# A hybrid decoder step on one core: convolution and gate at projection eviction, second-dilation keys in residue order, four stationary columns for the denominators

## The chip, the cores and the metric

The kernel runs on one core of a Trainium2 chip. The metric is the device time of one execution in microseconds (us), lower is better. The kernel before took 2710.33 us (median of three runs, 2706.25 to 2712.09). A profiled execution gives, for each engine, when each instruction ran and what it waited for. The engines are PE (TensorE: matmuls, and PEld for the weight loads that run beside them), DVE (VectorE), ACT (ScalarE), POOL (GpSimd) and SP, which here issues most DMA transfers. Each works off its own instructions strictly in order.

## The reference

One step of a decoder layer: 2048 new prompt tokens (and 64 sample tokens, which the change hardly touches). A combined projection feeds two branches: attention over three dilations (window 128 step 1, 512 step 4, 2048 step 16), and a state-space branch (a causal convolution of width 4, SiLU, then chunks of 128 tokens). Both are merged by an output projection and followed by an MLP.

```python
q, k, v, z, xbc, dt_raw = jnp.split(rmsnorm(h, norm_mix) @ w_in, IN_SPLITS, axis=-1)
groups = [dilated_group_prompt(q, k, v, d, w // d) for (w, d) in ((128, 1), (512, 4), (2048, 16))]
att = combine_groups(groups)                 # softmax over the union of the three windows
y = conv_b
for tap in range(4):                         # causal convolution along the tokens
    y = y + ext[:, tap:tap + s] * conv_w[tap]
xbc = silu(y)                                # x, B, C of the state-space branch
y, h_final = ssd_chunked(x, dt, A, B, C, h0) # 16 chunks of 128 tokens, one state carried over
y = (y + d_skip * x) * silu(z)               # z's gate, then a grouped RMS norm
h = h + concat([att, ssm]) @ w_out
h = h + (relu(rmsnorm(h) @ w_up) ** 2) @ w_down
```

## The kernel before, in words

All data is fp32. A large matmul is done as three: operands are split into a high part (rounded on ACT) and a low part (the rest, subtracted on DVE), and high x high, high x low and low x high are summed (`mm3`, lines 177 to 181; `mm`, lines 1124 to 1127). A scheduler orders the instructions of each engine when the program is built: it takes them by priority, which is the order of the code, but an instruction whose inputs or whose buffer are not yet there is passed over. That order is then fixed, and a tile's buffer can be used again when all readers of the former tile are done. So the code's order, the number of buffers and the place of a pool in memory together set the queues.

The work comes in five stretches.

1. **First projections** (lines 284 to 432). Eight blocks of 256 tokens give q, k, v and z. `z_part` computes four tiles of z per block, copies them from PSUM (L425) and stores them raw to `xz_s[8:12]` from ACT's queue (L426). Tiles `ev` and `kf` share two buffers.
2. **Attention** (the loop of 16 steps, 4 key heads x 4 blocks `s` of 512 tokens). `att_a` computes scores: `qk` (L609) multiplies keys, split in `kA` and `kB`, with queries. Dilation 1 takes 128 adjacent keys as the stationary operand, dilation 4 takes every fourth key (`slice(t0, t0 + 4 * 127 + 1, 4)`), dilation 16 every sixteenth (`att_qk3`). `att_b` subtracts the maximum, exponentiates, splits, sums the denominators by a matmul (`den_mm`, L696, which multiplies 128 columns of `rows_r`, only some of them ones, with 512 probabilities) and multiplies with the values (L749). `att_c` does the third dilation's values (L780) once per head. The other projection tiles, `ps_xz` (x, B and C: 8 tiles of 128 channels for each of the 8 blocks, `g2`), are placed between the attention matmuls as filler, held back by the table `STEP`; the last `LATE = 6` blocks of tiles 4 to 7 are code of the stretch after attention. `g2` copies a tile from PSUM (L811) and stores it raw.
3. **Hand-over**. The denominators are stored, loaded again (`dent`, L909), added, inverted and stored (`r_s`, L914); `merge` loads the attention outputs (`am`, L1060) and the inverses (`rd`, L1064), adds and multiplies them (L1073 to L1078) and splits the result into `mix`.
4. **First four chunks** of the state-space branch (`branch(0, ...)`), with the rest of the filler. `ssd_load` loads a chunk's raw x, B, C with three tokens of history (`xc`), the decays (`ar`), z (`zt`) and `ea`, two buffers each. `ssd` convolves on ACT and DVE (one ACT instruction L958 and three DVE instructions L960 for each of 8 channel tiles), applies SiLU (L970 tanh, L971), gates z (L972 tanh, L973), transposes (`ps_xt`, L977), multiplies the decays with C x B (L993), computes `ps_y` (L997), updates the state (`hst`), adds the skip (L1023), multiplies with the gate (L1024, POOL), norms (L1027 to L1041, matmuls `ps_ss` L1033 and L1038) and splits into `mix`.
5. **Output projection and MLP** (`out`, `up`, `down`), four passes of 512 tokens, from the first `ps_o` that needs the merged `mix`. The other twelve chunks and the sample tokens run beside the MLP's matmuls.

## Time and profile before

| of the profiled execution | value |
|---|---|
| its own time; its span in the trace | 2705.8 us; 2704.1 us |
| PE busy | 2582.9 us (96%) |
| DVE busy | 1650.8 us (61%) |
| ACT busy | 1146.5 us (42%) |
| POOL busy | 471.8 us (17%) |
| matmuls | 15382 |
| mean granted clock of PE | 0.979 |
| DMA, mean over the span | 172 GB/s |

Busy time is the time in which an engine executes. Matmuls are pipelined, so a busy PE can still have matmuls follow each other at different pitches; the pitch, start to start, is what a matmul costs. The chain that ended last is 69% PE. A wait is put down to the last thing that released it.

### The profile page before, as it was taken

How to read it: one execution, taken by the hardware profiler on the slowest of the kernel's cores; microseconds unless marked ns; L12 is line 12 of the kernel's file. 1: busy time of each engine (PE TensorE's matmuls, PEld its weight loads, DVE VectorE, ACT ScalarE, POOL GpSimd, SP SyncE). 2: the span in 40 equal slices, each digit the busy share in tenths (PEclk: the TensorE clock that was granted, in tenths of full speed). 3: DMA queues.
4: the chain of work that ended last, by engine and by line, in shares of the span. 5: the costliest groups of instructions: out<-in, count | busy, mean ns of one | idle time of the engine just before them, and what ended most of it. 6: DMA issues, size and time to landing. Idle time of an engine off the chain costs nothing.

```text
span 2704.1 us, 42090 instructions
## 1 busy us (share of the span) xinstructions
PE 2582.9 (96%) x15382; PEld 2268.9 (84%) x15382; DVE 1650.8 (61%) x2917; ACT 1146.5 (42%) x2203; POOL 471.8 (17%) x406
## 2 busy tenths in 40 slices
PE   7999789989956999999999999999999999999998
PEld 7999789989955777888888887777788889999998
DVE  6444357777767646777558775445667664555455
ACT  5334234555543434444454443343444434333333
POOL 2222124545612110010121010020000113000000
PEclk9999899999977999999999999999999999999999
DMA  7666768876693744544465446476644434433322
GB/s 262 190 207 211 206 204 238 223 233 186 210 261 97 224 133 156 160 146 139 164 210 168 149 141 196 159 227 221 187 141 153 148 119 146 161 102 103 109 98 86
DMA packets 346942, 464.56 MB, mean 172 GB/s; under 512 B 39264, under 2 KB 227104, under 8 KB 345696
## 3 DMA queue, kind: packets, MB, share of 16 engines
q1 hardware_dynamic: 302992, 425.24, 50.6%
q10 hardware_dynamic: 43744, 36.65, 4.2%
q8 instruction: 121, 1.98, 0.3%
q14 instruction: 85, 0.70, 0.1%
HBM read 366.25 MB, written 129.09 MB: 183 GB/s over the span
## 4 chain that ended last, share of the span: by engine, by line
PE 69%; DMA 3%; DVE 1%; issue 1%; ACT 0%; POOL 0%; SPq 0%; DVEq 0%; POOLq 0%; ACTq 0%
PE ps_dn L1124 9%; PE ps_up L1124 9%; PE ps_up L1126 9%; PE ps_dn L1127 9%; PE ps_dn L1126 9%; PE ps_up L1127 9%; PE ps_o L1124 2%; PE ps_o L1126 2%; PE ps_o L1127 2%; PE ps_po L1570 1%; PE ps_xz L177 1%; PE ps_xz L180 1%; PE ps_xz L181 1%; PE ps_yo L1003 1%; PE ps_y L997 0%
## 5 line engine op out<-in xcount | busy, mean ns | idle before, releaser
L899 ACT ACTIVATE wm_h<-raw_m 128x512 fp32r<-128x512 f32 x576 | 362.3, 630 | 791.8 <-PE ps_dn L1126 442.1
L900 DVE TENSOR_TENSOR wm_l<-raw_m,wm_h 128x512 fp32r<-128x512 f32 x576 | 415.7, 723 | 106.9 <-ACT wm_h L899 95.9
L1124 PE MATMUL ps_up<-xh_m,wm_h 128*128 128x512 f32 (+1 forms) x1280 | 458.5, 358 | 0.0
L1124 PE MATMUL ps_dn<-uh,wm_h 128*128 128x512 f32 (+1 forms) x1280 | 458.2, 359 | 0.0
L1126 PE MATMUL ps_up<-xl_m,wm_h 128*128 128x512 f32 (+1 forms) x1280 | 456.9, 357 | 0.0
L1126 PE MATMUL ps_dn<-ul,wm_h 128*128 128x512 f32 (+1 forms) x1280 | 456.8, 357 | 0.0
L1127 PE MATMUL ps_dn<-uh,wm_l 128*128 128x512 f32 (+1 forms) x1280 | 456.6, 357 | 0.0
L1127 PE MATMUL ps_up<-xh_m,wm_l 128*128 128x512 f32 (+1 forms) x1280 | 455.4, 356 | 0.0
L1244 DVE TENSOR_TENSOR acc<-acc,ps_dn 128x512 f32<-128x512 f32 (+1 forms) x320 | 189.5, 593 | 221.3 <-PE ps_dn L1127 218.8
L1124 PEld LDWEIGHTS ps_dn<-uh,wm_h 128*128 128x128 f32 x1280 | 240.4, 188 | 37.0 <-issue 4.3
L1127 PEld LDWEIGHTS ps_dn<-uh,wm_l 128*128 128x128 f32 x1280 | 240.6, 188 | 36.7 <-issue 2.8
L1124 PEld LDWEIGHTS ps_up<-xh_m,wm_h 128*128 128x128 f32 x1280 | 241.0, 188 | 36.0 <-issue 2.7
L1127 PEld LDWEIGHTS ps_up<-xh_m,wm_l 128*128 128x128 f32 x1280 | 241.5, 189 | 35.2 <-issue 1.5
L1126 PEld LDWEIGHTS ps_up<-xl_m,wm_h 128*128 128x128 f32 x1280 | 240.9, 188 | 35.0 <-issue 2.7
L1126 PEld LDWEIGHTS ps_dn<-ul,wm_h 128*128 128x128 f32 x1280 | 240.4, 188 | 34.5 <-issue 1.5
L1232 DVE SCALAR_TENSOR_TENSOR r<-ps_up,rs 128x512 f32<-128x512 f32 (+1 forms) x160 | 95.5, 597 | 158.6 <-PE ps_up L1127 157.4
L177 PE MATMUL ps_xz<-xq,wh 128*128 128x256 f32 (+1 forms) x512 | 148.7, 290 | 14.6 <-DMA xq<-xn_s 10.0
L1235 DVE TENSOR_TENSOR ul<-r,uh 128x512 fp32r<-128x512 f32 (+1 forms) x160 | 96.7, 604 | 94.4 <-ACT uh L1234 94.4
L180 PE MATMUL ps_xz<-xq,wh 128*128 128x256 f32 (+1 forms) x512 | 147.9, 289 | 0.0
L181 PE MATMUL ps_xz<-xq,wl 128*128 128x256 f32 (+1 forms) x512 | 147.3, 288 | 0.0
L1233 ACT ACTIVATE r<-r 128x512 f32<-128x512 f32 (+1 forms) x160 | 88.7, 555 | 110.3 <-DVE r L1232 109.9
L609 PE MATMUL ps_qk<-qt,kA 128*128 128x256 f32 x300 | 103.5, 353 | 20.9 <-DMA qt<-q_s 14.3
(356 smaller groups left out, 5136.5 us busy)
## 6 DMA issues: line engine op xcount, KB each, us to landing
raw_m<-wup SPq DMA_DIRECT2D x256, 256.0 KB
raw_m<-wdn SPq DMA_DIRECT2D x256, 256.0 KB
xq<-xn_s SPq DMA_DIRECT2D x48, 512.0 KB
am<-o_s SPq DMA_DIRECT2D x128, 128.0 KB
raw_m<-wout SPq DMA_DIRECT2D x64, 256.0 KB
ks<-ck SPq DMA_DIRECT2D x32, 510.0 KB
vs<-cv SPq DMA_DIRECT2D x32, 510.0 KB
xz_s<-ev ACTq DMA_DIRECT2D x96, 128.0 KB
```

The source lines that it names most:

```text
L177: r = nc.tensor.matmul(ps, wh(kk), xh(kk), start=kk == 0, stop=False)
L180: nc.tensor.matmul(ps, wh(kk), xl(kk), start=False, stop=False)
L181: k.zl = nc.tensor.matmul(ps, wl(kk), xh(kk), start=False, stop=kk == KT - 1)
L609: k.mm = nc.tensor.matmul(ov, kt[:, ksl], mv, start=first, stop=False, skip_group_check=True)
L899: k.at["ACT"] = nc.scalar.activation(hi, raw, AF.Copy)
L900: nc.vector.tensor_tensor(lo, raw, hi.bitcast(F32), op=ALU.subtract)
L1124: behind(nc.tensor.matmul(ps, wh[:, kk], xh(kk), start=first and kk == 0, stop=False), after)
L1126: nc.tensor.matmul(ps, wh[:, kk], xl(kk), start=False, stop=False)
L1127: r = nc.tensor.matmul(ps, wl[:, kk], xh(kk), start=False, stop=last and kk == nk - 1)
L1232: nc.vector.scalar_tensor_tensor(r, ps, 0.0, c(X.rs), op0=ALU.max, op1=ALU.mult)
L1235: nc.vector.tensor_tensor(c(ul), r, c(uh).bitcast(F32), op=ALU.subtract)
L1244: k.at["DVE"] = nc.vector.tensor_tensor(h, h, ps, op=ALU.add)
```

## The change

It has three parts, and moves memory and loads to make room for them.

**Convolution and gate at eviction.** `z_part` now applies z's gate to the tile before it is stored (tanh on ACT, one DVE instruction), for all 8 blocks; its store goes by SP's queue instead of ACT's (the name `'zg'` is not in `AQ`). In `g2`, blocks 0 and 1 (the first 512 tokens, chunks 0 to 3) are convolved and passed through SiLU in the tile `ex` that holds the evicted tile behind three tokens of history (`tl` carries the three last tokens from block 0 to block 1); the result goes to a new scratch `cv_s` by SP. `ssd` takes chunks 0 to 3 from there (`raw` is false), and no chunk gates z any more.

**Keys in residue order.** `att_a` copies each 512 keys, high and low, by ACT into `kr`, ordered by residue, and dilation 4 takes 128 adjacent columns of it.

**Denominators.** `rows_r` shrinks from 224 to 8 columns, and `den_mm` loads 4 of them as the stationary operand instead of 128; the 4 rows of the result are what is copied and stored.

Besides: `W4` is 3 instead of 4 (the buffers that `M`, `O12` and `O3` share), the pool `hst` is opened after attention, `ssd_load(0, ...)` stands ahead of the denominators' loads, and with two buffers the next chunk's loads are issued at a chunk's first yield instead of its seventh.

```diff
-W4 = 4
+W4 = 3
...
                 nc.scalar.activation(ev, ps, AF.Copy)
-                dq('z').dma_start(xz_s[8 + m, :, i * BS:(i + 1) * BS], ev[:, :BS])
+                th = gp.tile([P, NBX], F32, tag="t1", name="thz")[:, :BS]
+                nc.scalar.activation(th, ev[:, :BS], AF.Tanh, scale=0.5)
+                nc.vector.scalar_tensor_tensor(ev[:, :BS], th, 1.0, ev[:, :BS], op0=ALU.add, op1=ALU.mult)
+                dq('zg').dma_start(xz_s[8 + m, :, i * BS:(i + 1) * BS], ev[:, :BS])
...
+        kr = at.tile([P, 2, SB], F32R, tag="kr", name="kr", bufs=2)
+        for j, t in enumerate((G_.kA, G_.kB)):
+            nc.scalar.activation(kr[:, j].rearrange("p (r j) -> p r j", r=4),
+                                 t[:, s * SB:(s + 1) * SB].bitcast(F32).rearrange("p (j r) -> p r j", r=4), AF.Copy)
+        G_.kr = {**getattr(G_, "kr", {}), s: kr}
...
-                            t0 = (s - prev) * SB + c
-                            items.append((slice(t0, t0 + 4 * 127 + 1, 4), chunk2(qv, c), bank2(ps)[:, :, :, e]))
+                            items.append(([G_.kr[s - prev][:, j, c * P:c * P + P] for j in range(2)], chunk2(qv, c),
+                                          bank2(ps)[:, :, :, e]))
...
-            nc.tensor.matmul(ps, rows_r[:, w:w + P], t, start=j == 0 and t is hi, stop=j == 3 and t is lo, skip_group_check=True)
+            nc.tensor.matmul(ps[:4], rows_r[:, 3 - j:7 - j], t, start=j == 0 and t is hi, stop=j == 3 and t is lo, skip_group_check=True)
...
             nc.scalar.activation(ev, ps, AF.Copy)
-            dq('xz').dma_start(xz_s[m, :, i * BS:(i + 1) * BS], ev[:, :BS])
-            if i < 2:
+            if i > 1:
+                dq('xz').dma_start(xz_s[m, :, i * BS:(i + 1) * BS], ev[:, :BS])
+            else:
                 dq('xz').dma_start(xzs_s[m, :, i * DS:(i + 1) * DS], ev[:, BS:])
+                cx_ = yp.tile([P, BS], F32, tag="cvx", name="cvx", bufs=CVB)
+                nc.scalar.activation(cx_, ev[:, :BS], AF.Identity, scale=convw[:, m, 3:4], bias=convb[:, m:m + 1])
+                nc.vector.tensor_copy(tl[:, m], ex[:, BS:BS + 3])
+                for tap in range(3):
+                    nc.vector.scalar_tensor_tensor(cx_, ex[:, tap:tap + BS], convw[:, m, tap:tap + 1], cx_,
+                                                   op0=ALU.mult, op1=ALU.add)
+                th = ev[:, :BS]
+                nc.scalar.activation(th, cx_, AF.Tanh)
+                nc.vector.scalar_tensor_tensor(cx_, th, 1.0, cx_, op0=ALU.add, op1=ALU.mult)
+                dq('cvx').dma_start(cv_s[m, :, i * BS:(i + 1) * BS], cx_)
...
+        if c < 4:
+            xc = te.tile([P, 8, P], F32, tag="cv", name="cv", bufs=nb)
+            nc.sync.dma_start(xc, cv_s.rearrange("m p t -> p m t")[:, :, c * P:(c + 1) * P])
...
+    L0 = ssd_load(0, nc, te0, NBC)
     cx = ExitStack()
...
+        raw = c >= 4
+        cv = te.tile([P, 8, P], F32, tag="cv", name="cv", bufs=nb) if raw else xc
...
-        nc.scalar.activation(y, zt, AF.Tanh, scale=0.5)
-        nc.vector.scalar_tensor_tensor(f1(zt), f1(y), 1.0, f1(zt), op0=ALU.add, op1=ALU.mult)
...
-                if p == 6 and j < 3:
+                if p == (0 if nb > 1 else 6) and j < 3:
                     L = ssd_load(c + 1, nc, te, nb)
```

How this moves the queues shows at three places. The lines in the rows are those of the respective kernel.

First DVE, where attention ends and the first chunk begins. Before (`lo` is the last split of attention, `dent` the denominators, `cv` the convolution, `am` the merge, `xdt` the first use of the transposed chunk):

```order
L104 TENSOR_TENSOR lo_7233<-S_6322,hi_7232 128x512
L930 MEMSET xc 128x8x3
L912 TENSOR_TENSOR dent_8514<-dent_8514,dent_8515 128x128
L912 TENSOR_TENSOR dent_8514<-dent_8514,dent_8516 128x128
L913 RECIPROCAL dent_8514<-dent_8514 128x128
L960 SCALAR_TENSOR_TENSOR cv<-xc,convw,cv 128x128 x17
L973 SCALAR_TENSOR_TENSOR zt<-y,zt 128x512
L960 SCALAR_TENSOR_TENSOR cv<-xc,convw,cv 128x128 x3
L1074 TENSOR_TENSOR am<-am 128x512
L960 SCALAR_TENSOR_TENSOR cv<-xc,convw,cv 128x128 x4
```

The same place now:

```order
L105 TENSOR_TENSOR lo_7375<-S_6455,hi_7374 128x512
L1012 TENSOR_TENSOR xdt<-ps_xt,dtv 128x512
L1013 TENSOR_TENSOR xw<-ps_xt,wend 128x512
L1024 TENSOR_TENSOR ar<-ar,ps_bt 128x512 x2
L968 TENSOR_TENSOR dent_8820<-dent_8820,dent_8821 128x128
L968 TENSOR_TENSOR dent_8820<-dent_8820,dent_8822 128x128
L969 RECIPROCAL dent_8820<-dent_8820 128x128
L1105 TENSOR_TENSOR am<-am 128x512
L1054 SCALAR_TENSOR_TENSOR y<-cv,dskip,y 128x128 x4
L1108 TENSOR_TENSOR am<-am 128x512
L1109 TENSOR_TENSOR am<-am,rd 128x16x32
L1065 TENSOR_SCALAR rc_s<-ps_ss 128x2
```

The 24 convolution instructions of chunk 0 are gone, its `xdt` and `ar` moved ahead of the denominators, and the merge's product with `rd` (L1109) stands ahead of chunk 0's norm (`rc_s`).

Second SP's queue in the last steps of attention, between a step's first value load `V1` and its next, `dV1`. Before (`xq` are loads for the filler):

```order
L674 DMA V1_6933<-v3_s_82 128x4x128
L797 DMA xq_8913<-xn_s4_71 128x4x256
L797 DMA xq_8915<-xn_s4_71 128x4x256
L797 DMA xq_9147<-xn_s5_72 128x4x256
L797 DMA xq_9149<-xn_s5_72 128x4x256
L676 DMA dV1_6935<-v3_s_82 128x4x128
```

Now, in the step before that one (the last but one):

```order
L682 DMA V1_6912<-v3_s_82 128x4x128
L690 DMA V3_6920<-v3_s_82 128x16x128
L804 DMA xq_8975<-xn_s3_70 128x4x256
L937 DMA cv_8808<-cv_s_85 128x8x128
L942 DMA ar_8810<-ac_s_4052 128x1024
L947 DMA zt_8812<-xz_s_83 128x4x128
L951 DMA ea_8814<-ac_s_4052 64x4x128 x2
L937 DMA cv_8957<-cv_s_85 128x8x128
L942 DMA ar_8959<-ac_s_4052 128x1024
L947 DMA zt_8961<-xz_s_83 128x4x128
L684 DMA dV1_6914<-v3_s_82 128x4x128
```

The loads of chunks 0 and 1 moved from behind the denominators' loads to this place inside attention, ahead of value loads of the last two steps.

Third SP's queue where the first projections end and attention's keys are loaded. Before:

```order
L414 DMA v3_s_82<-vhl_3676 128x1536
L404 DMA v<-vf_3713 128x256
L414 DMA v3_s_82<-vhl_3717 128x1536
L546 DMA m3_4044<-m3 128x256
L549 DMA mf_4046<-m1 128x512
L549 DMA mf_4049<-m2 128x512
L599 DMA kA_4059<-k_s0_78 64x2x512
```

Now:

```order
L431 DMA xz_s_83<-ev_3982 128x256
L431 DMA xz_s_83<-ev_4013 128x256
L431 DMA xz_s_83<-ev_4044 128x256
L550 DMA m3_4138<-m3 128x256
L553 DMA mf_4140<-m1 128x512
L553 DMA mf_4143<-m2 128x512
L602 DMA kA_4152<-k_s0_78 64x2x512
```

The last eight stores of gated z tiles (three are shown) came into this queue, ahead of the first keys.

99 lines of the change are left out of this document (53 added, 46 removed).

## Prediction

> **What bounds the kernel now.** I read the chain of waits first, for the engine that sets the end.
>
> ```profile
> PE 69%; DMA 3%; DVE 1%; issue 1%; ACT 0%; POOL 0%; SPq 0%; DVEq 0%; POOLq 0%; ACTq 0%
> ```
>
> It is PE. So an edit pays where PE's matmuls follow each other too slowly, or where PE waits. Next I asked for the busy time by stretch (start and end, length, then each engine's busy time with its instructions, PE's granted clock, the share of the DMA engines, GB/s): first projections, way into attention, attention in two pieces, hand-over with the first four chunks, the rest.
>
> ```profile
> core 0: us, PE busy (x) PEld busy (x) DVE busy (x) ACT busy (x) POOL busy (x), PEclk, DMA share, GB/s
> 0.00:320.00 320.00, 302.05 (x2436) 297.92 (x2436) 148.13 (x322) 134.98 (x312) 71.66 (x90) 1.00 0.69 212
> 320.00:344.60 24.60, 8.80 (x46) 8.16 (x46) 9.87 (x16) 6.38 (x11) 2.51 (x2) 0.65 0.95 275
> 344.60:400.00 55.40, 48.42 (x313) 48.17 (x313) 28.13 (x35) 16.80 (x31) 12.57 (x6) 0.94 0.63 183
> 400.00:757.60 357.60, 340.70 (x2335) 328.19 (x2334) 262.09 (x295) 190.78 (x336) 185.47 (x128) 0.97 0.76 223
> 757.60:874.50 116.90, 65.41 (x419) 56.51 (x417) 83.34 (x191) 47.80 (x116) 27.85 (x23) 0.75 0.59 164
> 874.50:2704.10 1829.60, 1817.52 (x9838) 1530.01 (x9838) 1119.19 (x2060) 749.77 (x1403) 171.72 (x157) 1.00 0.48 153
> ```
>
> PE is idle for 51.5 of the 116.9 us between attention and output projection, for 23.9 of the 413 us of attention, and for only 12.1 of the last 1829.6. For the 116.9 us I then read PE's waits (what it worked on, what released it: total, times, longest) and its timeline, with one row of DVE's (start, duration).
>
> ```profile
> PE ps_ss L1033 <- POOL sq L1028: 15.5, 4, 6.6
> PE ps_xt L977 <- DVE cv L971: 15.4, 1, 15.4
> PE ps_y L997 <- DVE ar L993: 8.7, 2, 8.4
> ```
> ```profile
> 757.27 0.29 PE L780 MATMUL ps_pv<-lo,V 128*128 128x256 f32 x1
> 780.82 1.02 DVE L1078 TENSOR_TENSOR am<-am,rd 128x512 f32<-128x512 f32 x1
> 782.95 1.11 PE L977 MATMUL ps_xt<-ident,cv 128*128 128x128 f32 x4 [15.40 <-DVE cv L971]
> 840.04 1.09 PE L977 MATMUL ps_xt<-ident,cv 128*128 128x128 f32 x4
> 856.31 1.09 PE L977 MATMUL ps_xt<-ident,cv 128*128 128x128 f32 x4
> 868.70 1.01 PE L1033 MATMUL ps_ss<-ones_r,sq 128*128 128x1 f32 x4 [5.36 <-POOL sq L1028]
> 874.57 0.79 PE L1124 MATMUL ps_o<-mix,wm_h 128*128 128x512 f32 x1 [1.88 <-ACT mix L103]
> ```
>
> The longest wait, 15.4 us, is for the convolved first chunk, and that is due in 782.95, 25.7 us after the last value product. The first output matmul that needs all four chunks stands at 874.57.
>
> **The first four chunks.** Removed between 757.6 and 874.5 are these groups (count, busy, mean ns) and three smaller ones:
>
> ```profile
> L960 DVE SCALAR_TENSOR_TENSOR cv<-xc,convw,cv 128x128 f32<-128x128 f32 x96 | 31.1, 388 | 1.5 <-ACT cv L958 1.4
> L971 DVE SCALAR_TENSOR_TENSOR cv<-xc,cv 128x1024 f32<-128x1024 f32 x4 | 4.9, 1220 | 0.4 <-ACT xc L970 0.2
> L958 ACT ACTIVATE cv<-xc,convb,convw 128x128 f32<-128x128 f32 x32 | 12.7, 480 | 8.3 <-DMA xc<-xz_s 5.3 <-DMA raw_m<-wout 3.1
> ```
>
> That is 36 us of DVE's 83.3 and 12.7 of ACT's 47.8 busy time, so DVE is no longer near full here. The 15.4 us wait goes too: `cv` is loaded inside attention. What is late next is the merge, which the change leaves: in DVE's new queue the product with `rd` stands ahead of chunk 0's norm. In the trace of before it starts at 780.82, 23.5 us after the last value product, and nothing in its chain (store of the denominators, load, inverse, store, load) is removed. So I place chunk 0's norm there, and let three chunks follow at the pitch of chunks that are convolved in advance. Its ends are 856.31 − 840.04 = 16.3 us (two chunks' `ps_xt`) and 868.70 − 856.31 = 12.4 us (from the last chunk's `ps_xt` to its norm). From the last norm to `ps_o` it is 874.57 − 868.70 = 5.9. Sum: 23.5 + 3 x 12.4 + 5.9 = 66.6, or with 16.3, 78.3. I take 75, near the upper end, since the filler left for this stretch (264 matmuls instead of 239 by the two orders, some 31 us at 0.12) lies between the chunks' steps. Against 117 us that is **−42**, with −39 and −51 as ends. The transfers allow it: 164 GB/s x 116.9 us is 19.2 MB; at the 257 GB/s that the queues reach here,
>
> ```profile
> 800.00:820.00 20.00, 15.10 (x113) 14.50 (x112) 16.93 (x40) 11.05 (x28) 7.20 (x5) 0.91 1.02 258
> ```
>
> that takes 75 us, and 63 without the 3.1 MB that now load inside attention (of each chunk `cv` and `ar` at 0.52 MB, `zt` 0.26, two `ea` 0.13).
>
> **Attention: keys.** The scores of dilation 1 (adjacent keys) and 4 (every fourth) read like this, the weight loads below them:
>
> ```profile
> 395.03 0.27 PE L609 MATMUL ps_qk<-qt,kA 128*128 128x256 f32 x1
> 395.15 0.27 PE L609 MATMUL ps_qk<-qt,kB 128*128 128x256 f32 x1
> 401.18 0.40 PE L609 MATMUL ps_qk<-qt,kA 128*128 128x256 f32 x1
> 401.42 0.40 PE L609 MATMUL ps_qk<-qt,kB 128*128 128x256 f32 x1
> ```
> ```profile
> 400.47 0.19 PEld L181 LDWEIGHTS ps_xz<-xq,wl 128*128 128x128 f32 x1
> 401.28 0.33 PEld L609 LDWEIGHTS ps_qk<-qt,kB 128*128 128x128 f32 x1
> ```
>
> Same shape, a pitch of 0.12 against 0.24; and the load of every fourth column takes 0.33 where an adjacent one takes 0.19. Dilation 4 has 4 heads x (3 x 16 + 8) = 224 such matmuls: 224 x 0.12 = −26.9 us. The Trainium skill, "Advanced Engine Details and Errata", section "Memory Cachelines", says that SBUF is read in lines of 16 bytes and that an access which changes line each time costs extra; every fourth fp32 column is just that, and the two load rows agree with it.
>
> Its cost stands ahead of the scores: 16 steps x 2 copies of 128x512 on ACT. I price a copy by the row of a high part's rounding (same shape on ACT, 0.63); the other end is 0.63 x 1028/683 = 0.95, by the two merge products, whose slower one reads `rd` out of line.
>
> ```profile
> L103 ACT ACTIVATE hi<-S 128x512 fp32r<-128x512 f32 x96 | 59.8, 628 | 49.8 <-PE ps_pv L749 19.6 <-PE ps_pv L780 18.3 <-DMA qt<-q_s 7.2
> L1077 DVE TENSOR_TENSOR am<-am 128x512 f32<-128x512 f32 x4 | 2.7, 683 | 2.2 <-POOL am L1073 2.2
> L1078 DVE TENSOR_TENSOR am<-am,rd 128x512 f32<-128x512 f32 x4 | 4.1, 1028 | 0.0
> ```
>
> That is 20 to 30 us of ACT.
>
> **Attention: convolution at eviction.** Each of 16 tiles of 256 tokens adds four DVE instructions and some small copies, priced by a DVE instruction of the projections, and two on ACT, priced by the eviction's copy:
>
> ```profile
> L254 DVE SCALAR_TENSOR_TENSOR xr<-xr,g_mix,ps_r 128x256 f32<-128x256 f32 x48 | 19.3, 474 | 3.9 <-PE ps_r L203 3.9
> L811 ACT ACTIVATE ev<-ps_xz 128x256 f32<-128x256 f32 x38 | 14.4, 380 | 13.9 <-PE ps_xz L181 13.5
> ```
>
> 16 x (4 x 0.474 + 0.15) is 33 us of DVE, 16 x 2 x 0.43 is 14 of ACT. DVE goes from 290 to 323 of 413 us, ACT from 208 to about 245: neither is full, yet both sit in the loop from scores to probabilities. The loads of chunks 0 and 1 (3.1 MB, 12 us at 257 GB/s) stand on SP between value loads; there the queue has room between two rows of the last step:
>
> ```profile
> 703.60 0.52 SPq L682 DMA_DIRECT2D V<-v_s  x1
> 710.11 0.88 SPq L676 DMA_DIRECT2D dV<-v_s  x1
> ```
>
> I take half of the 20 us of copies as exposed, and 2 of the 12 us of loads: −26.9 + 10 + 2 = **−15**. The ends: −27 if filler covers all; +5 if the 20 us of copies and the 12 of loads are wholly exposed.
>
> **Gate in the projections.** 32 tiles add 32 x 0.38 = 12 us on ACT and 32 x 0.474 = 15 on DVE. PE has 302 of 320 us there, DVE 148, ACT 135: **0**; with that cover gone it would be some 0.85 us a tile. At the end it isn't covered: eight gated stores now precede the masks and the first keys on SP,
>
> ```profile
> 318.05 0.81 SPq L549 DMA_DIRECT2D mf<-m  x2
> 318.92 0.57 SPq L599 DMA_DIRECT2D kA<-k_s  x1
> ```
>
> and the last of them needs copy, tanh and product, 0.38 + 0.38 + 0.47 = 1.2 us. Between 0 (landing decides) and +4 (that, and four stores queued at 0.7 each) I take **+2**.
>
> **Denominators.** The row is
>
> ```profile
> L696 PE MATMUL ps_den<-lo,rows_r 128*128 128x512 f32 x96 | 39.8, 415 | 3.2 <-DVE lo L104 3.2
> ```
>
> What streams is 512 probabilities, before and after; 4 instead of 128 stationary columns shorten only the load, which runs beside the stream: **0**. Output projection and MLP: PE 1817.5 of 1829.6 us, twelve gate products fewer on DVE behind it: **0**.
>
> **The sum.** The profiled execution took 2705.8 us (span 2704.1). −42 − 15 + 2 = −55 gives 2651; the median before, 2710.33, lies 4.5 above it, so 2655 is the forecast.
>
> **The rivals.**
>
> A. *Attention gives all of the keys' gain back.* What it would show: ACT's key copies released late, and scores waiting for them; both engines gain work in the same loop. Against it, PE idles only 6% there and filler stands by. Attention at 0 instead of −15: −40, 2670.
>
> B. *The hand-over binds the chunks.* The store, load, inverse, store, load of the denominators share the queues with more loads, and chunk 1 to 3 can't overtake the merge. Then half of the transition's gain is left: −21 − 15 + 2 = −34, 2676. For it: the DMA share is already 0.9 to 1.0 between 780 and 820. Against it: 3.1 MB leave that stretch.
>
> C. *The stride doesn't set the pitch.* If the load of weights cost the same in any layout and the 0.24 came from the queries' side, adjacent keys would stay at 0.24 and the copies' 12 us would be paid for nothing: −42 + 12 + 2 = −28, 2682. The rows with 0.33 and 0.19 for the load itself speak against it. The Trainium skill, "TensorE: Matmul & The Clock Gate", section "LDWEIGHTS (loading the stationary operand)", has such a rule: the time goes by the number of columns alone; by it the new order would bring nothing.
>
> D. *SP holds its queue for the convolved stores; slower than before.* SP works in order. Sixteen stores to `cv_s` now wait there at the end of a chain from PSUM through ACT, DVE, ACT and DVE, and behind them stand the loads of the next keys, values and filler. How long SP waits behind such a store today:
>
> ```profile
> SPq L760 <- ACT den L700: 24.2, 8, 7.2
> ```
>
> The longest is 7.2: 16 x 7.2 = 115 us of held queue. The change loses from 55/16 = 3.4 us on that PE really feels for each store. With all felt it is −55 + 115 = +60, 2770; with half, about +3. Against it: a convolved tile's whole chain, 3 x 0.38 on ACT and 4 x 0.474 on DVE, is 3.0 us, under the 3.4, and most steps leave PE other matmuls to do meanwhile.
>
> **How the numbers follow.** Chances: forecast 0.53, A 0.21, B 0.15, C 0.04, D 0.07. The forecast's own ends are −27 − 51 + 0 = −78 (2632) and +5 − 39 + 4 = −30 (2680). A, B and C lie inside, B with A's attention is −19 (2691). So 2632 to 2691 holds about 0.85 to 0.9 of it; what is outside is D and combinations of ends. Differences within 0.2% (5.4 us) can't be told from none. A, B, C and the forecast are all faster: 0.93; D gives 0.06 slower and 0.01 same.
>
> **What the profile after would show.** Right: dilation 4's score matmuls at a pitch near 0.12; `ps_xt` of chunk 0 within some 5 us of the last value product; from that product to `ps_o` on `mix` some 75 us; attention (first `ps_qk` to last value product) about 15 us shorter. Wrong: pitch still 0.24 (C); `ps_qk` waiting for `kr`, or DVE without gaps in the steps that convolve (A); `ps_ss` or `ps_o` waiting for `am` or `rd` (B); `xq` or value loads late on SP behind a `cv_s` store (D). The forecast fails if the transition stays above 95 us.

## The result, and the profile after

The changed kernel took 2694.87 us (median of four runs, 2693.51 to 2698.32) against 2709.14 us before (four runs beside it): ratio 0.9950, 95% interval 0.9935 to 0.9966. It is faster, by 14 us and not by the 55 of the forecast. The profiled execution has a span of 2691.8 us against 2704.1.

Cut at the same events in both traces, the span came out like this (us; the forecast's terms in the last column):

| stretch | before | after | difference | forecast |
|---|---|---|---|---|
| start to the last matmul of z | 317.7 | 327.2 | +9.5 | 0 |
| to the first score matmul | 16.4 | 18.8 | +2.4 | +2 |
| attention, to the last value product | 423.1 | 434.6 | +11.5 | −15 |
| to the first output matmul on the complete `mix` | 117.3 | 80.1 | −37.2 | −42 |
| rest | 1829.5 | 1830.9 | +1.4 | 0 |

The table of stretches of the changed kernel, cut at these events (start and end, length, busy time by engine, PE's granted clock, DMA share, GB/s):

```profile
core 0: us, PE busy (x) PEld busy (x) DVE busy (x) ACT busy (x) POOL busy (x), PEclk, DMA share, GB/s
0.00:327.60 327.60, 305.76 (x2436) 301.60 (x2436) 161.69 (x355) 145.86 (x342) 72.11 (x90) 0.99 0.66 207
346.00:781.00 435.00, 384.65 (x2666) 352.99 (x2667) 333.67 (x430) 257.21 (x452) 206.85 (x138) 0.94 0.77 220
781.00:860.80 79.80, 60.78 (x444) 54.64 (x443) 46.07 (x86) 23.69 (x58) 22.74 (x21) 0.88 0.75 212
```

And attention of the kernel before, cut in the same way:

```profile
334.10:757.60 423.50, 397.92 (x2691) 384.51 (x2692) 298.01 (x336) 213.53 (x373) 200.56 (x136) 0.96 0.75 221
```

After attention PE is idle for 19.0 of 79.8 us instead of 51.5 of 116.9, and DVE does 46 us of work there instead of 83. In attention it is the other way round: PE is busy 13 us less but idle for 50.3 us instead of 25.6.

PE's timeline of the changed kernel at the transition:

```profile
780.72 0.28 PE L787 MATMUL ps_pv<-lo,V 128*128 128x256 f32 x1
783.90 0.60 PE L1008 MATMUL ps_xt<-ident,cv 128*128 128x128 f32 x4
798.52 0.61 PE L1064 MATMUL ps_ss<-ones_r,sq 128*128 128x1 f32 x4 [3.06 <-POOL sq L1059]
860.85 0.80 PE L1155 MATMUL ps_o<-mix,wm_h 128*128 128x512 f32 x1 [1.88 <-ACT mix L104]
```

The first chunk's `ps_xt` follows 3.2 us behind the last value product (25.7 before), its norm 17.8 us behind it, and the output matmul 80.1. The keys also did what was foretold; these are the groups of the score matmuls by their stationary operand (count, duration in ns least/median/most):

```profile
L612 PEld LDWEIGHTS ps_qk<-qt,kr x224: 186/188/333, 349.0 to 717.2; 128*128 128x128 f32 x112
L612 PE MATMUL ps_qk<-qt,kr x224: 279/283/582, 349.2 to 717.3; 128*128 128x256 f32 x112
```

A load of reordered keys takes 0.188 us instead of 0.33, as it does for adjacent keys. Four such matmuls in a row read

```profile
716.92 0.65 PE L612 MATMUL ps_qk<-qt,kr 128*128 128x256 f32 x4
```

The last of the four takes 0.28 us, so they start 0.12 us apart, where 0.24 stood before. The 0 for the denominators held as well: a `ps_den` matmul takes 412 ns with 4 stationary columns and took 415 with 128. So the transition and the keys' pitch are there, and what is missing was lost in the projections and in attention. PE's waits in the changed kernel's attention, until 740 us (total, times, longest):

```profile
PE ps_xz L179 <- DMA xq<-xn_s: 13.7, 4, 6.3
PE ps_qk L612 <- DVE S L666: 8.5, 8, 2.0
PE ps_den L703 <- DVE lo L105: 5.9, 7, 1.8
PE ps_den L703 <- ACT hi L104: 5.2, 3, 4.0
PE ps_pv L756 <- DMA dV<-v_s: 4.7, 1, 4.7
```

Before, the first four of these were 8.4, 3.6, 3.2 and 3.0 us, and there was no wait for `dV`. No single wait of PE holds the loss; it is spread over the loop from scores to probabilities. What the third buffer does shows one step further back, on DVE: `M` shares its buffers with `O12` and `O3`, and waits until the store of an older `O` has landed. Before and now:

```profile
DVE M L686 <- DMA o_s<-O: 1.7, 1, 1.7
DVE M L694 <- DMA o_s<-O: 5.5, 3, 2.9
```

With the waits of this kind for `O` itself on ACT, it is 1.7 us before and 7.8 now. The kernels of this study with three buffers have 4.2 to 11.6 us of it, those with four 0.8 to 2.3.

### The profile page after: what moved, and what is told of

The parts are those of the page before. It is cut to its first block, busy times and chain, and to the rows that moved or that the text cites. A ratio compares the mean times of both kernels' runs of the same rounds, so it can differ in the third digit from the quotient of the medians.

```text
span 2691.8 us, 42208 instructions
## 1 busy us (share of the span) xinstructions
PE 2569.3 (95%) x15382; PEld 2239.4 (83%) x15382; DVE 1654.1 (61%) x2927; ACT 1175.7 (44%) x2247; POOL 475.1 (18%) x406
## 4 chain that ended last, share of the span: by engine, by line
PE 81%; DMA 7%; DVE 5%; issue 2%; SPq 2%; ACT 1%; POOL 1%; ACTq 0%; DVEq 0%; POOLq 0%
PE ps_dn L1155 9%; PE ps_up L1155 9%; PE ps_up L1157 9%; PE ps_dn L1158 9%; PE ps_dn L1157 9%; PE ps_up L1158 9%; PE ps_o L1158 2%; PE ps_o L1157 2%; PE ps_o L1155 2%; PE ps_qk L612 2%; DMA xq<-xn_s 2%; DMA o_s<-O 1%; PE ps_pv L756 1%; PE ps_qk L179 1%; PE ps_z L179 1%
## 5 line engine op out<-in xcount | busy, mean ns | idle before, releaser
L928 DVE TENSOR_TENSOR wm_l<-raw_m,wm_h 128x512 fp32r<-128x512 f32 x576 | 410.0, 713 | 110.9 <-ACT wm_h L927 100.5
L1157 PEld LDWEIGHTS ps_up<-xl_m,wm_h 128*128 128x128 f32 x1280 | 240.8, 188 | 35.2 <-issue 2.7
L179 PE MATMUL ps_qk<-xq,wh 128*128 128x256 f32 (+1 forms) x384 | 111.9, 293 | 9.2 <-DVE st L332 7.3
```

Of the source, the lines that this page charges most:

```text
L179: r = nc.tensor.matmul(ps, wh(kk), xh(kk), start=kk == 0, stop=False)
L928: nc.vector.tensor_tensor(lo, raw, hi.bitcast(F32), op=ALU.subtract)
L1157: nc.tensor.matmul(ps, wh[:, kk], xl(kk), start=False, stop=False)
```

## The experiments

Seventeen kernels were run. For all of them the table gives the time and, from the profile, the last matmul of z; the stretch from the first score matmul to the first output matmul on the complete `mix`; and how this stretch is made up: time in which PE works, PE idle in attention, PE idle after it. The ratio is to the kernel before on the same chip.

| kernel | time, us | ratio (95%) | last z | stretch | PE works | idle, attention | idle, after |
|---|---|---|---|---|---|---|---|
| before | 2709.1 | | 317.7 | 540.4 | 463.3 | 25.5 | 51.6 |
| changed | 2694.9 | 0.9950 (0.9935 to 0.9966) | 327.2 | 514.8 | 445.4 | 50.3 | 19.1 |
| 1 z raw | 2683.7 | 0.9908 (0.9895 to 0.9921) | 316.1 | 518.6 | 449.4 | 51.6 | 17.6 |
| 2 strided keys | 2711.6 | 1.0007 (0.9991 to 1.0022) | 329.2 | 533.5 | 467.0 | 42.1 | 24.3 |
| 3 plain key copy | 2696.7 | 0.9951 (0.9937 to 0.9964) | 330.2 | 514.2 | 445.1 | 51.3 | 17.8 |
| 4 convolution late | 2711.3 | 1.0011 (1.0001 to 1.0021) | 328.3 | 536.6 | 444.7 | 41.4 | 50.5 |
| 5 before, three buffers | 2709.0 | 0.9999 (0.9989 to 1.0010) | 318.2 | 542.1 | 469.4 | 41.7 | 31.0 |
| 6 before, adjacent keys | 2705.3 | 0.9982 (0.9972 to 0.9993) | 317.2 | 538.7 | 444.6 | 38.2 | 55.9 |
| 7 z raw, loads late | 2690.7 | 0.9931 (0.9918 to 0.9944) | 317.9 | 523.7 | 446.5 | 56.4 | 20.8 |
| 8 gate from PSUM | 2698.7 | 0.9962 (0.9950 to 0.9974) | 323.5 | 525.5 | 445.7 | 51.3 | 28.5 |
| 9 strided, four buffers | 2699.0 | 0.9964 (0.9951 to 0.9976) | 326.0 | 521.0 | 460.8 | 36.6 | 23.7 |
| 10 z raw by SP | 2698.5 | 0.9955 (0.9939 to 0.9971) | 325.8 | 524.4 | 451.1 | 52.2 | 21.1 |
| 11 z raw, tails on POOL | 2694.1 | 0.9942 (0.9924 to 0.9959) | 315.6 | 527.6 | 453.8 | 50.8 | 23.0 |
| 12 z raw, four buffers, three splits | 2708.4 | 0.9998 (0.9984 to 1.0012) | 317.0 | 542.6 | 454.1 | 63.3 | 25.2 |
| 13 gate, stored by ACT | 2704.5 | 0.9990 (0.9978 to 1.0001) | 327.4 | 522.6 | 445.9 | 47.9 | 28.8 |
| 14 z raw, strided, four buffers | 2685.4 | 0.9915 (0.9900 to 0.9930) | 317.7 | 512.6 | 461.2 | 33.6 | 17.7 |
| 15 z raw, half the keys, four buffers | 2687.4 | 0.9917 (0.9904 to 0.9931) | 316.8 | 522.1 | 456.3 | 45.0 | 20.8 |
| 16 three `kf`, one `dv` | 2690.1 | 0.9931 (0.9916 to 0.9946) | 324.0 | 514.9 | 445.5 | 51.2 | 18.2 |
| 17 one `dv` | 2693.9 | 0.9941 (0.9929 to 0.9953) | 329.4 | 516.3 | 443.9 | 53.2 | 19.2 |

An edit can change the order of the whole stretch: the filler matmuls left behind attention vary from 178 to 294 in these kernels. A difference of a few us in the stretch is therefore not read as the effect of the edited instructions alone. The stretches are also those of one profiled execution each, while the times of one kernel's executions lie 3.5 us (run 1) to 23.5 us (run 2) apart. Run 4's profiled execution was its slowest (2717.2 us), run 14's its fastest (2678.8).

### The first projections: 1, 8, 10, 13, 16, 17

**1, z raw.** z is stored raw from ACT's queue and gated in the chunks.

```diff
-                th = gp.tile([P, NBX], F32, tag="t1", name="thz")[:, :BS]
-                nc.scalar.activation(th, ev[:, :BS], AF.Tanh, scale=0.5)
-                nc.vector.scalar_tensor_tensor(ev[:, :BS], th, 1.0, ev[:, :BS], op0=ALU.add, op1=ALU.mult)
-                dq('zg').dma_start(xz_s[8 + m, :, i * BS:(i + 1) * BS], ev[:, :BS])
+                dq('z').dma_start(xz_s[8 + m, :, i * BS:(i + 1) * BS], ev[:, :BS])
...
+        nc.scalar.activation(y, zt, AF.Tanh, scale=0.5)
+        nc.vector.scalar_tensor_tensor(f1(zt), f1(y), 1.0, f1(zt), op0=ALU.add, op1=ALU.mult)
```

> The changed kernel with z stored raw from ACT's queue and gated in the chunks, as before the change. Theory: the gate at eviction keeps the two buffers of tag kf until SP's store has landed, ACT waits for one of them (25.6 us in 7 waits) and the evictions of q and k behind it come late, so PE lost 9.5 us in the first projections. Then the last matmul of z, at 327.2 us now, comes back to 317 to 319, the stretch after attention grows by 0 to 6 us (2.5 us of tanh on ACT, 3.4 us of products on DVE), and the time falls by 3 to 9 us from 2694.9. Rival: the loss in the projections has another cause (stores and small loads queued on SP in another order); then the last matmul of z stays at 325 or later and the time is the same or some us higher.

The last matmul of z came back to 316.1 and the time fell by 11 us, to 2683.7: the lowest median of this study (14 and 15 can't be told from it), 25 us under the one before. So the gate edit costs the projections about 10 us. How, this run does not say.

**10 and 13** take the edit's two halves apart. In 10, z is raw but stored from SP; in 13, z is gated but stored from ACT.

```diff
-                dq('z').dma_start(xz_s[8 + m, :, i * BS:(i + 1) * BS], ev[:, :BS])
+                dq('zg').dma_start(xz_s[8 + m, :, i * BS:(i + 1) * BS], ev[:, :BS])
```

> The kernel with z stored raw (2683.7 us, last matmul of z at 316.1), but stored from SP's queue instead of ACT's. If the gate's chain (copy, tanh, product, store) holds the two shared buffers too long, raw stores from SP cost nothing: last matmul of z at 315 to 318 and 2682 to 2686 us. If the place in SP's queue is what costs, the last matmul of z comes at 321 or later and the time at 2689 or more.

```diff
-AQ = ('xn', 'ac', 'o3', 'z', 'xz')
+AQ = ('xn', 'ac', 'o3', 'z', 'xz', 'zg')
```

> The changed kernel with the gated z tiles stored from ACT's queue instead of SP's, and nothing else. Raw z stored from SP cost as much as gated z from SP (last matmul of z at 325.8 and 327.2), so the queue and not the gate should be the cause. If so, the last matmul of z comes back to 316 to 319 with the gate still at eviction, and the time to 2681 to 2687. If the gate costs by itself as well, the last matmul of z stays at 321 or later.

The theory on the gate missed in 10 (last z at 325.8, not 315 to 318), and the theory on the queue missed in 13 (327.4, not 316 to 319). Each half alone brings nearly the whole loss in the projections. (By time run 13 is even 10 us slower than the changed kernel, and no run takes that apart: its order behind attention is another, with 212 filler matmuls left there instead of 264 and 28.8 us idle instead of 19.1.) What both halves have in common is that the two buffers of tag `kf`, which the z tiles share with the keys, come free later. ACT's longest waits for one of them, before and in the changed kernel:

```profile
ACT ev L425 <- DMA xz_s<-ev: 17.9, 9, 3.4
```
```profile
ACT ev L427 <- DMA xz_s<-ev: 27.1, 8, 6.5
```

The longest is 3.4 us with raw z from ACT (3.5 in run 1), and 6.5, 6.7 and 5.0 us in the changed kernel, 10 and 13. ACT works in order, so the tanh of the next z tile comes late too; DVE's gate product waits for that tanh, and behind the product on DVE stands the eviction of q from PSUM (`st`), for which PE waits. In the changed kernel (waits of DVE, then of PE):

```profile
DVE ev L430 <- ACT thz L429: 47.4, 19, 6.4
PE ps_qk L179 <- DVE st L332: 7.3, 3, 2.7
```

Of PE's three gaps the second and third (2.1 us at 188, 2.5 at 262) end such a chain: ACT waits 5.5 and 5.8 us for the buffer there, and DVE 6.1 and 6.5 for the tanh. In the first (2.7 us) DVE waits 3.4 us for a load of `convw`, with a gate product and the eviction of q behind it; before, a wait of 3.8 us for the same load brought no gap. (In run 10, without the gate, PE waits for ACT itself: for `dg`, 4.7 us in 2 waits.) PE is idle 4.8 us more than before in all (7.8 against 3.0 from 40 us to the last z). Most of the rest is the granted clock, which falls behind the first and the third gap. The table around the first (114.6 to 117.3), clock in the third column from the right:

```profile
112.00:117.20 5.20, 2.63 (x22) 2.42 (x21) 1.71 (x7) 2.91 (x8) 2.88 (x4) 1.00 0.34 79
117.20:121.00 3.80, 3.70 (x18) 3.73 (x19) 2.49 (x8) 0.65 (x1) 0.00 (x0) 0.55 0.20 54
121.00:125.00 4.00, 4.00 (x36) 4.00 (x35) 4.00 (x11) 2.58 (x5) 0.00 (x0) 1.00 0.00 0
```

Behind the gap the clock averages 0.55 over 3.8 us, in which 18 matmuls run instead of some 34.

**8, gate from PSUM.** ACT's copy is gone and ACT no longer waits for the buffer itself:

```diff
-                nc.scalar.activation(ev, ps, AF.Copy)
...
-                nc.scalar.activation(th, ev[:, :BS], AF.Tanh, scale=0.5)
-                nc.vector.scalar_tensor_tensor(ev[:, :BS], th, 1.0, ev[:, :BS], op0=ALU.add, op1=ALU.mult)
+                nc.scalar.activation(th, ps[:, :BS], AF.Tanh, scale=0.5)
+                nc.vector.scalar_tensor_tensor(ev[:, :BS], th, 1.0, ps[:, :BS], op0=ALU.add, op1=ALU.mult)
+                if i < 2:
+                    nc.scalar.activation(ev[:, BS:], ps[:, BS:], AF.Copy)
```

> The changed kernel with z's gate taken from PSUM: ACT writes the tanh straight from PSUM and DVE multiplies with PSUM into ev, so ACT no longer waits for one of the two buffers that SP's stores hold (only the 64 sample columns of the first two blocks are still copied), and one ACT instruction per tile is gone. If ACT standing in line for that buffer cost the projections their 9.5 us, the last matmul of z comes back from 327.2 to 316 to 321 us and the time to about 2684 to 2689. If the work of the gate or the order of SP's queue cost it, the last matmul of z stays over 324 us.

The last z came at 323.5, between the two: DVE now waits for the buffer (18.7 us in 7 waits), and ACT for DVE. The time did not follow (2698.7 against 2694.9): as in run 13, 212 filler matmuls are left behind attention, and PE is idle 28.5 us there.

**16 and 17** test the buffers themselves: a third one (the same number in all three places of the tag), paid for with one of `dv`, and the control with `dv` alone.

```diff
-                kf = gp.tile([P, NBX], F32, tag="kf", name="kf", bufs=2)[:, :n]
+                kf = gp.tile([P, NBX], F32, tag="kf", name="kf", bufs=3)[:, :n]
...
-                        src = gp.tile([P, NKV, HD], F32, tag="dv", name="dv", bufs=2)
+                        src = gp.tile([P, NKV, HD], F32, tag="dv", name="dv", bufs=1)
```

> The changed kernel with three buffers instead of two for the tag that z's tiles and the keys share in the projections (kf), paid for by one buffer instead of two for the small differences of the values (dv); gate and SP's stores are kept. If the shared buffers that come free too late are what both the gate and SP's queue cost the projections, the last matmul of z comes from 327.2 to 315 to 319 us and the time to 2681 to 2687. If it stays at 324 or later, and the run with dv alone isn't slower than the changed kernel, the buffers are not the cause.

> The control to the run with three buffers: the changed kernel with one buffer for dv and still two for kf. It should be as the changed kernel or some us slower: last matmul of z 327 to 332 us, time 2693 to 2700.

The control came at 329.4, the third buffer at 324.0: 5.4 us back, less than expected. All waits of `ps_qk` are gone; what PE waits for in run 16 from 40 to 330 us is one row, the values behind the single `dv`:

```profile
PE ps_z L179 <- ACT vf L399: 6.7, 4, 2.6
```

So the shared buffers cause a part of the loss, with gate and SP's stores kept; ACT's waits for the stores of `ev` fall from 20.6 us in run 17 to 8.8. How large a part stays open. The last z of kernels whose projections are the same (changed, 2, 3, 4 and 9) lies between 326.0 and 330.2, nearly as far apart as 16 and 17; the intervals of the times of 16 and 17 overlap; and the `dv` that paid for the third buffer brought waits of its own.

### The keys and what they displaced: 2, 3, 5, 6, 9, 14, 15

**2, strided keys; 3, plain copy.** In 2 the copies are left out and dilation 4 reads every fourth key again. In 3 the copies stay but leave out the reordering, so they read adjacent columns.

```diff
-                            items.append(([G_.kr[s - prev][:, j, c * P:c * P + P] for j in range(2)], chunk2(qv, c),
+                            t0 = (s - prev) * SB + c
+                            items.append(([t[:, t0:t0 + 4 * 127 + 1:4] for t in (G_.kA, G_.kB)], chunk2(qv, c),
```

> The changed kernel without the key copies: dilation 4 reads every fourth key again. Theory: the contiguous keys save PE some 21 us (score matmuls, 110.6 to 89.7 us from start to start), but 32 copies at 1.15 us are 36 us of ACT ahead of the scores and give most of it back; then attention (first score matmul to last value product, 434.6 us now) stays within 8 us. Rival A: the copies are hidden and the convolution alone ate the gain; then attention grows by 15 to 27 us and the time to 2710 to 2720. Rival B: the copies cost more than they bring; attention shrinks by over 8 us.

```diff
-            nc.scalar.activation(kr[:, j].rearrange("p (r j) -> p r j", r=4),
-                                 t[:, s * SB:(s + 1) * SB].bitcast(F32).rearrange("p (j r) -> p r j", r=4), AF.Copy)
+            nc.scalar.activation(kr[:, j], t[:, s * SB:(s + 1) * SB].bitcast(F32), AF.Copy)
```

> The changed kernel with the key copies made without reordering (adjacent columns in, adjacent columns out), so that dilation 4 multiplies wrong keys; everything else is kept. The copy should take 0.63 us instead of 1.15, 17 us less on ACT in attention. If ACT's copies ahead of the scores delay PE, attention (434.6 us now) shrinks by 5 to 15 us; if the loss sits in the convolution on DVE or in SP's queue, it changes by less than 3 us.

Strided keys lose 16.8 us, and the stretch grows by 18.7: the theory that the copies eat the gain fell. Run 3 points the same way: the copies, in the changed kernel and in run 3, are

```profile
L632 ACT ACTIVATE kr<-kA 128x512 fp32r<-128x512 f32 x14 | 16.1, 1152 | 5.6 <-PE ps_qk L612 5.5
L632 ACT ACTIVATE kr<-kB 128x512 fp32r<-128x512 f32 x15 | 17.2, 1144 | 0.0
```
```profile
L632 ACT ACTIVATE kr<-kA 128x512 fp32r<-128x512 f32 x16 | 10.0, 628 | 19.3 <-DMA kA<-k_s 14.5 <-PE ps_qk L612 4.7
```

0.63 us instead of 1.15, some 16 us of ACT, change neither attention (435.6 against 434.6) nor the time. What the copies still cost at 0.63 us no run separates.

**5, 6, 9: the third buffer.** The change took one of four buffers from `M`, `O12` and `O3`, to make room for the reordered keys. Run 5 makes that edit alone in the kernel before; run 6 adds the adjacent keys and the denominators to it, without convolution and gate; run 9 is run 2 with the fourth buffer back.

```diff
-W4 = 4
+W4 = 3
```

> The kernel before with three buffers instead of four for M, O12 and O3, and nothing else. Without the convolution attention is still 421 us with the adjacent keys, so something takes back what they bring; waits of PE for the copies into O (9.1 us, not there before) point to these buffers. If they are it, attention (423.1 us before) grows by 8 to 18 us and the time by as much, to 2717 to 2727; if not, both stay within 3 us.

> The kernel before with the keys in residue order, the 4 stationary columns and the memory that these need (three buffers, the pool of the state moved), without convolution or gate at eviction and with the chunks' loads where they were. If the keys alone bring what the pitch says and nothing in the memory costs, attention falls by 20 to 27 us to about 400 and the time to about 2687. If the three buffers or the copies cost, attention is 410 to 425 and the time 2695 to 2710. If attention is near 400 here, the early loads of the chunks are what keeps it at 421 with the late convolution.

```diff
-W4 = 3
+W4 = 4
```

> The changed kernel without the key copies (as in the run before of that kind, 2711.6 us) and, in the memory that this frees, four buffers instead of three for M, O12 and O3. From the first score matmul to the first output matmul on the merged mix that run took 533.5 us, 42.1 of it PE idle in attention. If the third buffer is what PE waits for also in the changed kernel, idle time in attention falls by 10 to 18 us, and with the convolution out of the way it isn't given back after attention: the stretch falls to 517 to 525 and the time to about 2696 to 2704. If the loss is only moved (as in the kernel before, where 16 us more idle in attention stood against 21 less after it), the stretch and the time stay within 4 us.

Run 5 in the table of stretches (attention, then to the output matmul):

```profile
334.50:782.50 448.00, 406.30 (x2698) 391.55 (x2699) 316.90 (x389) 228.35 (x412) 203.22 (x138) 0.94 0.74 219
782.50:876.60 94.10, 63.08 (x413) 55.12 (x411) 65.24 (x139) 31.95 (x77) 24.40 (x21) 0.80 0.55 157
```

and attention in run 6:

```profile
336.00:753.00 417.00, 378.83 (x2695) 353.02 (x2696) 292.63 (x336) 240.11 (x402) 200.29 (x136) 0.95 0.78 224
```

In run 5 attention grew by 25 us. Of these PE is idle for 16 and works 8.6 us longer on nearly the same matmuls, at a clock of 0.94 instead of 0.96. But the stretch grew only by 1.7 and the time not at all: work of the first chunk on DVE that used to follow attention (83.3 us there, 65.2 now) moved into its gaps. My expectation of 8 to 18 us on the whole kernel missed; that for attention was too low. In run 6 the keys cut PE's busy time in attention from 406 to 379 us against run 5, as much as the forecast's 26.9, yet the time is only 4 us under the kernel before: behind attention PE then waits 55.9 us, where the convolution still is.

Once the convolution has moved, nothing gives the buffer's price back: run 9 against run 2 is 12.7 us faster (2699.0 against 2711.6), with a stretch shorter by 12.5. The idle time in attention fell by only 5.5 us, though, where 10 to 18 were expected; 6.2 us are PE's shorter work, at a clock of 0.91 instead of 0.80 behind attention.

**14 and 15.** 14 is run 1 with strided keys and four buffers (the edits of 2 and 9). 15 is run 1 with one buffer of reordered keys instead of two, for the current block only, and with four buffers.

> The kernel with z stored raw from ACT, strided keys as before the change and four buffers for M, O12 and O3. From the changed kernel the strided keys lost 16.8 us, and the fourth buffer then gave 12.7 back (2694.9, 2711.6, 2699.0), so the adjacent keys with the memory that they take are worth some 4 us. If this holds with z raw as well, 2683.7 + 4 = 2686 to 2690; if keys and buffers act on each other, it falls outside.

```diff
-        kr = at.tile([P, 2, SB], F32R, tag="kr", name="kr", bufs=2)
+        kr = at.tile([P, 2, SB], F32R, tag="kr", name="kr", bufs=1)
...
+                            ws = [t[:, t0:t0 + 4 * 127 + 1:4] for t in (G_.kA, G_.kB)] if prev else \
+                                 [kr[:, j, c * P:c * P + P] for j in range(2)]
```

> The kernel with z stored raw, with one buffer of reordered keys instead of two, so that only the current block's 128 of 224 dilation-4 matmuls read adjacent keys (the block before is read with a stride again), and the memory given to a fourth buffer for M, O12 and O3. Of the 16.8 us of the keys 128/224 stay, so 7.2 are lost, and 12.7 are won by the buffer: 2683.7 + 7.2 - 12.7 = 2678, within 2674 to 2682. If the single buffer of keys makes the scores wait for one another, 2685 or more.

14 took 2685.4 us, just under the 2686 to 2690 expected, against 2683.7 of run 1; the intervals of the two overlap. In the stretch PE works 11.8 us more and is idle 17.9 us less. So adjacent keys with three buffers and strided keys with four can't be told apart by time here: what the keys save in matmuls, their memory costs in waits. The same pair with the gate, the changed kernel and run 9, is 4 us apart, and those intervals overlap too. 15, which should have kept over half of the keys' gain and had the fourth buffer as well, took 2687.4, outside the expected 2674 to 2682. Its PE time lies between (456.3), its idle time in attention (45.0) nearer to three buffers; a copy that must wait for the scores of the step before could do that, but this was not tried.

### Convolution, loads and two attempts: 4, 7, 11, 12

**4, convolution late.** The first 512 tokens are stored raw and convolved in the chunks.

```diff
-            if i > 1:
+            if True:
                 dq('xz').dma_start(xz_s[m, :, i * BS:(i + 1) * BS], ev[:, :BS])
-            else:
+            if i < 2:
                 dq('xz').dma_start(xzs_s[m, :, i * DS:(i + 1) * DS], ev[:, BS:])
+            if False:
                 cx_ = yp.tile([P, BS], F32, tag="cvx", name="cvx", bufs=CVB)
...
-        raw = c >= 4
+        raw = True
```

> The changed kernel with the first 512 tokens stored raw and convolved in the chunks, as before the change; keys, denominators, gate and the place of the chunk loads are kept. Theory: the convolution at eviction (46 us more on DVE, 16 on ACT, in two bursts where DVE is 94 to 98% busy) cost attention most of what the keys saved, so attention falls from 434.6 to 400 to 412 us, and the stretch from the last value product to the first output matmul on the merged mix (80.1 us now) grows to 100 to 117; the time is within 10 us of 2695. Rival: the loss comes from the key copies or the early chunk loads; then attention stays over 425 us and the time rises to 2715 or more.

The stretch from the last value product grew to 115.3 us as expected. Attention fell to 421.3, not to 412 or less, and the time rose by 16 us to 2711.3, which was not expected. So moving the convolution earns 21.8 us in the stretch: 31.4 less idle time behind attention, 8.9 more in it. The price shows where the first eight tiles are convolved, 34 to 74 us into attention; the same piece of the changed kernel and of run 4:

```profile
380.00:420.00 40.00, 35.74 (x272) 33.94 (x270) 37.59 (x60) 27.08 (x48) 18.31 (x9) 1.00 0.81 212
```
```profile
382.00:422.00 40.00, 40.00 (x313) 38.73 (x312) 29.67 (x35) 26.48 (x43) 20.72 (x11) 1.00 0.85 228
```

With the convolution DVE is busy for 37.6 of 40 us and PE is idle for 4.3; without it DVE has room and PE is never idle.

**7, loads late.** Run 1, with the chunks' loads behind the denominators' loads again and the next chunk's at the seventh yield.

```diff
-    L0 = ssd_load(0, nc, te0, NBC)
     cx = ExitStack()
...
     dq('rs').dma_start(r_s.rearrange("g s (a b) -> (g s a) b", b=P), dent)
+    L0 = ssd_load(0, nc, te0, NBC)
...
-                if p == (0 if nb > 1 else 6) and j < 3:
+                if p == 6 and j < 3:
```

> The kernel with z stored raw (2683.7 us), and the chunks' loads put back behind the denominators' loads and to the seventh yield. If the early loads hold up the queue for attention's own loads, attention (436.3 us there) falls by 5 to 15 us; the stretch to the first output matmul on the mix (82.3 us) grows by 5 to 20 us, since the chunks wait for their loads. If they do not, attention stays within 3 us and the time rises by 5 to 20 us.

7 us slower than run 1, and attention isn't shorter (443.4 against 436.3): the early loads don't hold up attention, and they pay. Not in the place expected, though: the stretch behind attention didn't grow (80.3 against 82.3), and attention did, with 239 filler matmuls left behind it instead of 277.

**11 and 12.** 11 is run 1 with the copies of the last three tokens, and the tiles' start columns (a copy or a memset), on POOL; 12 is run 1 with four buffers for `M` and `O`, paid for by three for `hi` and `lo`.

```diff
-                nc.vector.tensor_copy(tl[:, m], ex[:, BS:BS + 3])
+                nc.gpsimd.tensor_copy(tl[:, m], ex[:, BS:BS + 3])
```

> The kernel with z stored raw, and the copies of the three last tokens of each convolved tile (24 on DVE, 0.42 and 0.29 us each, 9 us) made by POOL. If DVE's bursts are what the convolution costs attention, PE's idle time in attention (51.6 us) falls by 2 to 6 us and the time (2683.7) by as much; if not, both stay within 2 us.

```diff
-HB = 4
+HB = 3
...
-W4 = 3
+W4 = 4
```

> The kernel with z stored raw, with four buffers for M, O12 and O3, paid for by three instead of four for the split probabilities (hi and lo). If the third buffer of M and O is the tightest, PE's idle time in attention (51.6 us) falls by 5 to 15 us and the time to 2670 to 2679; if the split probabilities are tighter, it grows and the time is 2685 or more.

Both missed. 11 was 10 us slower though DVE had less to do (320.5 us busy in attention against 332.5): idle time in attention hardly moved, PE worked 4.4 us more and was idle 5.4 us more behind it; I have no cause for it that a run shows. 12 was 25 us slower, with 11.7 us more idle time in attention: the split probabilities are tighter than `M` and `O`.

## Why the prediction was wrong

**Direction, bound and transition held.** PE sets the end, the kernel got faster, and the transition gave 37.2 of the forecast 42 us. Chunk 0's norm did come together with the merge's product, half a microsecond before it, but the product came 18.3 us behind the last value product instead of 23.5: I took its chain for unchanged, and overlooked that before 20 convolution instructions stood ahead of the merge in DVE's queue. The chunks' pitch was too short: `ps_xt` at 783.90 and the next ones 15.1, 18.9 and 22.4 us apart, where 12.4 to 16.3 were taken; the leftover filler runs between them. The first error made 5.7 us, the second some 11 the other way, so that the term came out close is partly luck. Rival B, the hand-over as the bound, didn't come about.

**The steps that failed most: two terms of attention that I put at nothing.** The change lists `W4` 4 to 3, and the sum had no term for it. I worked out the convolution's work on DVE and ACT, saw that neither is full, and charged nothing for it. Three of the kernels lead from before to after, one part of the change at a time, so the forecast of attention can be held against them (us; one execution each, in this order only):

| edit, run | attention | difference | forecast |
|---|---|---|---|
| before | 423.1 | | |
| third buffer instead of four (5) | 447.9 | +24.8 | no term |
| keys and denominators (6) | 416.9 | −31.0 | −16.9 |
| gate and early loads (4) | 421.3 | +4.4 | +2 |
| convolution (changed) | 434.6 | +13.3 | no term |

The buffer and the convolution make 38.1 us where nothing was charged, and the keys bring 14.1 more than forecast. A price in attention is not yet one of the kernel. Nearly all of the buffer's 24.8 us came back after attention as long as the convolution stood there (run 5, same time as before); without it, and with strided keys, 12.7 us of time hang on the buffer (run 9 against run 2). The convolution's 13.3 us are repaid by 35.2 behind attention. Runs 1 and 14 show that the keys, with the memory that they need, bring nothing that can be measured.

**The keys' own term held.** PE works 27.5 us less in attention with them (run 6 against run 5), where −26.9 was forecast, so rival C is out. That before and after differ by only 13.2 us of busy time there is the 8.6 that the third buffer adds by the lower clock, and 4.5 that came with the convolution (run 4 against the changed kernel). The rule of the Trainium skill on weight loads ("TensorE: Matmul & The Clock Gate", "LDWEIGHTS (loading the stationary operand)"), by which only the number of columns counts, does not hold for these loads: 128 columns each, 0.33 us with a stride of four and 0.188 without.

**The copies' price was wrong and mattered little.** They take 1.15 us, beyond both ends of the bracket (0.63 and 0.95), and I charged 10 us for them. Run 3 shows that 16 us of ACT less change nothing, and the keys' step in the table came out better than a forecast without any charge.

**Rival A**, attention gives the gain back, is what happened, but by another mechanism than I gave it (key copies released late): by the buffer and the convolution. The price of the convolution's instructions was right for an undisturbed one: half of the taps take 0.478 us or less and half of the small copies 0.160 or less. But means of 0.619 and 0.416 made it 46 us instead of 33. All 11 of the 48 taps that took over 0.56 us ran beside an instruction of POOL, and 9 of the 37 others did.

**The projections' 0 was wrong.** The busy times that I rested it on say that DVE and ACT have room, and they have. What had none were two buffers: ACT's wait for one of them, 17.9 us in 9 waits, stood in the trace of before. Lengthening either half of what holds the buffer costs some 10 us up to the last z (9.7 in run 10 and 11.3 in run 13, against run 1); in the changed kernel 4.8 are more idle time of PE, and 3.4 an estimate for two times 3.4 us at half the clock. How much of it the buffers make by themselves stays open (runs 16 and 17). The price that I named for a lost cover, 0.85 us a tile, was a price of work, not of a buffer held.

**Rival D** (SP held by stores) was near in the projections, where z from SP costs 10 us (run 10), by buffers that come free late. In attention the waits on `xq` and `dV` grew by some 7 us together; with the chunks' loads late (run 7) the one for `dV` is gone and the one for `xq` nearly as long as in run 1 (15.1 us, 16.2 there), and run 7 is slower all the same. What the `cv_s` stores by themselves cost there wasn't tried.

## What to carry to other kernels

Price what pays for an edit as carefully as the edit: here a buffer taken from another tile cost waits in a loop in which DVE, ACT and POOL had room, and the next stretch's slack hid that price until the slack was removed. Ask of each tile that is held longer who needs its buffer next, on an in-order engine, and look for waits on that buffer that the trace already shows. The contiguous copy of the keys saved 27 us of PE's work in attention, and the memory that it took gave them back.

## What the runs showed of the hardware

- ACT reads every fourth fp32 column at 1.15 us for 128x512, adjacent ones at 0.63 (run 3); the Trainium skill's rule on lines of 16 bytes ("Advanced Engine Details and Errata", "Memory Cachelines") agrees with this, as with the weight loads.
- Behind a gap of 2.7 us between matmuls PE's granted clock was 0.50 from 117.5 to 120.8 us, and behind one of 2.5 us (at 262) 0.50 from 264.3 to 267.6; behind one of 2.1 us (at 188) it stayed at 1.00. The length of the gap doesn't decide it alone: 1.8 us at 171.5 in run 16 was followed by 0.50 (173.9 to 177.2), 2.8 us at 263.9 in run 4 by 1.00 (266.8 to 271). The Trainium skill ("TensorE: Matmul & The Clock Gate", "Part 1: The HAM clock gate") gives an idle window of about 3.4 us; here shorter gaps were enough.
- On DVE a mean can hide two kinds of instruction. The convolution's taps (128x256) have a mean of 619 ns and a median of 478, and the copies of 128x3 a mean of 416 and a median of 160; every tap over 0.56 us ran beside POOL, and the longest, 2.11 us, lay wholly within POOL's reduction of `M`. Least, median and longest in ns:

```profile
L832 DVE SCALAR_TENSOR_TENSOR cvx<-ev,convw,cvx x48: 460/478/2108, 373.4 to 692.6; 128x256 f32<-128x256 f32 x48
L830 DVE COPY tl<-ev x16: 149/160/1552, 370.7 to 685.3; 128x3 f32<-128x3 f32 x16
```

The groups with their means:

```profile
L832 DVE SCALAR_TENSOR_TENSOR cvx<-ev,convw,cvx 128x256 f32<-128x256 f32 x48 | 29.5, 619 | 2.6 <-ACT cvx L829 2.3
L836 DVE SCALAR_TENSOR_TENSOR cvx<-ev,cvx 128x256 f32<-128x256 f32 x16 | 7.5, 468 | 0.0
L830 DVE COPY tl<-ev 128x3 f32<-128x3 f32 x16 | 6.7, 416 | 1.5 <-ACT ev L823 1.5
```
